# A hybrid decoder trunk on one core: the S5 loop's tile products moved to the end of the iteration, the next tile's matrix products put behind two weight units

## The chip, the core and the metric

The kernel runs on one core of one Trainium2 chip. The metric is device time in microseconds (us) of one execution; lower is better. The time before is 1483.97 us, the median of 3 runs (1483.57 to 1484.95). Engines are named as in the profile: PE (TensorE; PEld is its weight loads), DVE (VectorE), ACT (ScalarE), POOL (GpSimd) and SP (SyncE), which issues all of the kernel's DMAs.

## What is computed

One layer is applied to a prompt of 512 tokens and to 8 samples of 4 tokens, 544 columns in all. The normed input is projected to four branches of width 1024 (A: Mamba-2 SSD, B: S5, C: mLSTM, D: cross-attention); each branch goes through its own down projection, the four are merged by gates, and an output projection and a last norm follow. The change lies in branch B, the S5 scan: 64 groups of 16 channels with a complex state of 64 each.

```python
lam_bar = jnp.exp(lam * dt)
b_bar = ((lam_bar - 1.0) / lam)[..., None] * lax.complex(b_re, b_im)
bu = jnp.einsum('gnc,btgc->btgn', b_bar, ug)      # 16 channels -> 64 states
bu = bu.at[:, 0].add(lam_bar * h0)
h = lax.associative_scan(combine, (a_el, bu))      # h_t = lam_bar h_(t-1) + bu_t
y = jnp.einsum('gcn,btgn->btgc', c, h).real + d_skip * u
y = gelu(y)
```

## The kernel before, in words

**Weight units.** Nearly all of the matrix work is done by `unit` (the matmuls stand on L188): one unit multiplies 128 output columns of a weight with all 544 columns of the activations. A float32 product is made of three products of rounded parts, so a unit has 8 x 3 x 2 = 48 matmuls of 128x272. SP loads the weight block into `raw` (512 KB, three buffers), ACT rounds it into `whi` (L177), DVE subtracts to get `wlo` (L64), PE multiplies into the PSUM tile `pu` (two buffers). `gate_down` is a generator of such units: a gate unit (input `xh`, `xl`), then a down unit (input `oh`, `ol`) whose result DVE multiplies into `merged`. `step(gd, n)` runs n of them.

**The S5 loop** handles the 64 groups in 8 tiles f = 0..7 of 8 groups (128 channels), with the time axis cut into 64 chunks of 8 steps. Its parts, with the tiles that the profile names:
- `s5_in(f)`: one unit for the input columns of tile f; ACT and DVE copy `pu` to `uf`, which goes to DRAM (`ud`) and back as `U` in another layout (two DMAs).
- `s5_mats(f)`: DVE and POOL build the matrices `bm` (input to state) and `cm` (state to output); PE transposes `bm` into PSUM (`pbt`, L739), ACT and DVE copy that to `bt`; PE multiplies `cm` with `bbs` (`pk`, L768) for the short convolution inside a chunk, ACT copies it to `kt`, which goes to DRAM (`kd`) and back as `tp`.
- `s5_scan(f)`: PE makes `pvr` and `pvi` from `U` and `bt` (L791, 32 matmuls); DVE and POOL rotate them by the phases `E` (`gr`, `gi`, `t`), scan (L807, L808), rotate back to `hs`, and add the sample states to `hn`, which is the last reader of `pvr` and `pvi`.
- `s5_y(f)`: PE makes `py` from `tp` and `U` and from `cm` and `hs` (L846, L847, 32 matmuls); ACT copies `py` to `yj` (the same buffer as `uf`), which goes to DRAM (`yd`) and back as `yt`.
- `s5_out(f)`: PE permutes `yt` into PSUM (`pn`, L858 to L860); ACT and DVE apply the GELU to the stage tile `st`.
- `s5_rot(q)`, after the even iterations 0, 2 and 4: POOL alone builds the phases of the tiles 2q and 2q+1 by doubling (`rt`, `st`).

The small PSUM tiles (`pvr`, `pvi`, `pbt`, `pk`, `py`, `pn`) share four banks. The program builder hands the instructions to the engines by a timing model, so the order in the program is near that of the code but not the same, and matmuls of a unit stand on both sides of smaller work. Each engine then runs its own instructions strictly in that order.

Before, one iteration is written: scan of f, matrices of f+1, output of f-1, one unit of `gd`, `s5_y` of f, the input unit of f+2, one more unit of `gd` (none at f = 0 and f = 5).

Of the kernel before, what the change touches and what calls it, by code (L numbers as in the profile page):

```python
# [8 lines left out]
F32 = mybir.dt.float32  # L9
# [7 lines left out]
P = 128  # L17
# [17 lines left out]
def hybrid_kernel(ctx: ExitStack, tc: tile.TileContext, I, O):  # L35
    nc = tc.nc
    V, G, S, T = nc.vector, nc.gpsimd, nc.scalar, nc.tensor
# [7 lines left out]
    def ctile(shape, name, dt=F32):  # L45
        return cst.tile(shape, dt, name=name, tag=name)

    def bank(name="bk"):
        return pst.tile([P, 512], F32, name=name, tag="bk")
# [7 lines left out]
    def copy(eng, out, in_):  # L57
        if eng is S:
            S.copy(out, in_)
        else:  # L60
            eng.tensor_copy(out, in_)
# [39 lines left out]
    ident = ctile([P, P], "ident")  # L101
# [134 lines left out]
    def step(gen, n=1):  # L236
        for _ in range(n):
            next(gen, None)
# [4 lines left out]
    for c in range(5):  # L243
        n = P if c < 4 else TS
# [46 lines left out]
    pb = bank("pb")  # L291
# [11 lines left out]
    pb = bank("pb")  # L303
# [39 lines left out]
    for c in range(2):  # L343
# [8 lines left out]
        for hb in range(2):  # L352
            pb = bank("pmt")
# [4 lines left out]
            f = xm0.tile([P, 4, P], F32, name="mf", tag="mf")  # L358
# [71 lines left out]
    for b in range(NB):  # L430
# [10 lines left out]
        for h in range(4):  # L441
            kt_ = xk.tile([P, 2, 256], F32, name="kbt", tag="kbt", bufs=6)
            kts.append(kt_)
            pb = bank("pkt")
# [17 lines left out]
    pb = bank("pps")  # L462
# [51 lines left out]
    NV = 80  # L514
# [171 lines left out]
    pb = bank("pxo")  # L686
# [12 lines left out]
    s5r = s5c.enter_context(tc.tile_pool(name="s5r", bufs=1, side="right", reuse_waits="tile"))  # L699
# [8 lines left out]
    def s5_in(f):  # L708
        pu = unit(wcols(C_U + f * P), x2, perm=True)
        uf = s5r.tile([P, 8, NV], F32, name="uf", tag="uf", bufs=1)  # L710
        G.memset(uf[:, 4:8, 0:8], 0.0)
        G.memset(uf[:, 0:4, 72:80], 0.0)
        S.copy(uf[:, :, 8:42], pu[:, 0, 0:272].rearrange("p (k s) -> p s k", s=8))
        S.copy(uf[:, :, 42:72], pu[:, 1, 0:240].rearrange("p (k s) -> p s k", s=8))
        us = pu[:, 1, 240:272].rearrange("p (b t) -> p t b", t=4)
        V.tensor_copy(uf[:, 0:4, 0:8], us)
        V.tensor_copy(uf[:, 4:8, 72:80], us)
        U = s5r.tile([P, 8, NV], F32, name="U", tag="U", bufs=2)
        ud = s5d.tile([8, P, NV], F32, name="ud", tag="ud")
        dma(ud.rearrange("q p k -> p q k")[:, ::-1], uf)  # L720
        dma(U, ud.rearrange("q (c g) k -> (q c) g k", g=8))

        return U

    def s5_mats(f):
        gs = slice(4 * f, 4 * f + 4)

        def e4(a, m):
            return bc(a[:, 0:m, gs].rearrange("p l a -> p a l"), 3, 16)
        bm = s5r.tile([P, 2, 4, 8, 16], F32, name="bm", tag="bm")  # L730
        q1 = s5r.tile([P, 4, 9, 16], F32, name="q1", tag="sc1")
        q2 = s5r.tile([P, 4, 9, 16], F32, name="q2", tag="sc2")
        bbrf, bbif = bc(bbr[:, gs, :], 2, 8), bc(bbi[:, gs, :], 2, 8)
        cmul(V, G, bm[:, 0], bm[:, 1], e4(pwr, 8), e4(pwi, 8), bbrf, bbif, q1[:, :, 0:8, :], q2[:, :, 0:8, :])
        bt = s5r.tile([P, 2, 4, P], F32, name="bt", tag="bt")
        for ri in range(2):
            pb = bank("pbt")
            for a in range(4):
                T.transpose(pb[:, a * P:(a + 1) * P], bm[:, ri, a].rearrange("p l c -> p (l c)"), ident)  # L739
            copy(S if ri else V, bt[:, ri].rearrange("p a n -> p (a n)"), pb)  # L740

        cm = s5r.tile([P, 8, 9, 16], F32, name="cm", tag="cm", bufs=2)
        cmv = cm.rearrange("p (a b) l c -> p a b l c", b=2)
        ctrf, ctif = bc(ctr[:, gs, :], 2, 9), bc(cti[:, gs, :], 2, 9)
        q1 = s5r.tile([P, 4, 9, 16], F32, name="q1", tag="sc1")
        q2 = s5r.tile([P, 4, 9, 16], F32, name="q2", tag="sc2")
        tt(G, q1, e4(pwr, 9), ctrf, MUL)
        tt(V, q2, e4(pwi, 9), ctif, MUL)
        for g2 in range(2):
            pr = slice(64 * g2, 64 * g2 + 64)  # L750
            tt(V, cmv[0:64, :, g2], q1[pr], q2[pr], SUB)
        q1 = s5r.tile([P, 4, 9, 16], F32, name="q1", tag="sc1")
        q2 = s5r.tile([P, 4, 9, 16], F32, name="q2", tag="sc2")
        tt(G, q1, e4(pwi, 9), ctrf, MUL)
        tt(G, q2, e4(pwr, 9), ctif, MUL)
        for g2 in range(2):
            pr = slice(64 * g2, 64 * g2 + 64)
            stt(cmv[64:128, :, g2], q1[pr], -1.0, q2[pr], MUL, SUB)

        bbs = s5r.tile([P, 4, 2, 16], F32, name="bbs", tag="bbs", bufs=2)  # L760
        for ri, src in enumerate((bbr, bbi)):
            for g2 in range(2):
                dma(bbs[64 * ri:64 * ri + 64, :, g2, :], src[64 * g2:64 * g2 + 64, gs])

        pk = bank("pk")
        for g2 in range(2):
            for a in range(4):
                T.matmul(pk[32 * a:32 * a + 32, g2 * P:(g2 + 1) * P], bbs[:, a].rearrange("p g c -> p (g c)"),  # L768
                         cm[:, 2 * a + g2, 0:8, :].rearrange("p l c -> p (l c)"), start=True, stop=True,
                         tile_position=(0, 32 * a))  # L770
        kt = s5r.tile([P, 2, P], F32, name="kt", tag="kt")
        S.copy(kt.rearrange("p g x -> p (g x)"), pk[:, 0:256])
        stt(kt[:, :, 0:16], bc(i16, 1, 2), dcol[:, f:f + 1], kt[:, :, 0:16], MUL, ADD)

        kd = kds[f % 2]
        for a in range(4):
            dma(kd[:, a, :, 112:240], kt[32 * a:32 * a + 32])
        tp = [s5r.tile([P, 4, P], F32, name="tp", tag=f"tp{g2}", bufs=2) for g2 in range(2)]
        for g2 in range(2):
            dma(tp[g2], bass.AP(tensor=kd.tensor, offset=kd.offset + g2 * (16 * 1920 + 240),  # L780
                                         ap=[[16, 8], [1920, 16], [480, 4], [1, P]]))
        return bt, cm, tp, ev_[f // 2][:, :, f % 2]

    def s5_scan(f, U, bt, E):
        gs = slice(4 * f, 4 * f + 4)

        pv = [bank("pvr"), bank("pvi")]
        for g in range(8):
            pr = slice(64 * (g % 2), 64 * (g % 2) + 64)
            for ri in range(2):  # L790
                T.matmul(pv[ri][pr, (g // 2) * 72:(g // 2) * 72 + 72], bt[:, ri, g // 2, pr], U[:, g, 8:80],  # L791
                         start=True, stop=True)
# [44 lines left out]

    def s5_y(f, U, cm, tp, hs_):

        yj = s5r.tile([P, 8, 72], F32, name="yj", tag="uf")  # L840
        for hb in range(2):
            py = bank("py")
            for g4 in range(4):
                g = 4 * hb + g4
                o = py[:, g4 * 72:(g4 + 1) * 72]
                T.matmul(o, tp[g % 2][:, g // 2, :], U[:, g, 0:72], start=True, stop=False)  # L846
                T.matmul(o, cm[:, g, 1:9, :].rearrange("p l c -> p (l c)"), hs_[:, g, 0:72], start=False, stop=True)  # L847
            S.copy(yj[:, 4 * hb:4 * hb + 4, :].rearrange("p g k -> p (g k)"), py[:, 0:288])
        yt = s5r.tile([P, 8, 72], F32, name="yt", tag="yt")
        yd = s5d.tile([P, 8, 72], F32, name="yd", tag="yd")  # L850
        dma(yd, yj)
        dma(yt, yd.rearrange("(j c) g k -> (c g) j k", c=16))
        return yt
# [12 lines left out]
            S.activation(ga, ga, AF.Tanh)  # L866
            stt(ga, ga, 1.0, y, ADD, MUL)

    us_, mt_, yt = [s5_in(0)], s5_mats(0), None
    step(gd)  # L870
    us_.append(s5_in(1))
    step(gd)
    for f in range(8):
        bt, cm, tp, E = mt_
        hs_ = s5_scan(f, us_[f], bt, E)
        if f < 7:
            mt_ = s5_mats(f + 1)
        if f > 0:
            s5_out(f - 1, yt)
        step(gd)  # L880
        yt = s5_y(f, us_[f], cm, tp, hs_)
        if f < 6:
            us_.append(s5_in(f + 2))
        step(gd, (0, 1, 1, 1, 1, 0, 1, 1)[f])
        if f % 2 == 0 and f // 2 + 1 in range(1, 4):
            s5_rot(f // 2 + 1)
    s5_out(7, yt)
# [43 lines left out]
    with tc.tile_pool(name="sd", bufs=1, side="right", reuse_waits="tile") as sd:  # L931
# [199 lines left out]
        for q in range(3):  # L1131
            cvr = sr.tile([24, 512], F32, name="cvr", tag="M", bufs=1)
            dma(cvr, I["state_ssd_conv"][0].rearrange("b j c -> (b j) c")[:, q * 512:(q + 1) * 512])
            pb = bank("pcv")
# [33 lines left out]
        for g in range(2):  # L1168
            pb = bank("pbt")
# [3 lines left out]
            pb = bank("pcb")  # L1173
# [8 lines left out]
        for j in range(8):  # L1182
# [8 lines left out]
            pb = bank("pxt")  # L1191
# [9 lines left out]
            for h2 in range(2):  # L1201
                h = 2 * j + h2
                pb = bank("pac")
# [47 lines left out]
        for q in range(3):  # L1251
            pb = bank("pco")
# [28 lines left out]
        for g in range(2):  # L1281
            pb = bank("pbs")
# [10 lines left out]
        pb = bank("pms")  # L1293
# [9 lines left out]
        for hb in range(2):  # L1303
            pb = bank("pxs")
# [22 lines left out]
        for b in range(NB):  # L1327
# [5 lines left out]
            bm = sr.tile([96, 2, P], F32R, name="bmk", tag="bmk")  # L1333
# [5 lines left out]
            for hb in range(2):  # L1339
# [3 lines left out]
                pb = bank("pso")  # L1343
# [4 lines left out]
            for hb, so in enumerate(sos):  # L1348
                tt(G, so, so, bc(decS[:, 4 * hb:4 * hb + 4, b], 2, P), MUL)
                pb = bank("psn")  # L1350
# [7 lines left out]
        for qd in range(4):  # L1358
# [3 lines left out]
            for j in (2 * qd, 2 * qd + 1):  # L1362
                o = py[:, j * TS:(j + 1) * TS]
                a = 2 * (j % 2)
# [16 lines left out]
        pb = bank("pss")  # L1381
        for c in range(5):
            n = P if c < 4 else TS
# [6 lines left out]
        pb = bank("prb")  # L1390
# [4 lines left out]
        pb = bank("prb")  # L1395
# [13 lines left out]
    with tc.tile_pool(name="mlr", bufs=1, side="right", reuse_waits="tile") as mr:  # L1409
        for h in range(4):  # L1410
# [24 lines left out]
            for c in range(4):  # L1435
                sl = slice(c * P, (c + 1) * P)
                pb = bank("pkv")
# [42 lines left out]
            for dt in range(2):  # L1480
# [3 lines left out]
                pb = bank("pht")  # L1484
# [10 lines left out]
            pb = bank("pss")  # L1495
# [14 lines left out]
    with tc.tile_pool(name="mss", bufs=1, side="right", reuse_waits="tile") as ms:  # L1510
# [9 lines left out]
        for hb in range(2):  # L1520
            pb = bank("pk4")
# [16 lines left out]
        pb = bank("pqs")  # L1538
# [19 lines left out]
        pb = bank("pnr")  # L1558
# [5 lines left out]
        for b in range(NB):  # L1564
# [14 lines left out]
            for hb, cb in enumerate(cbs_):  # L1579
                for a in range(4):  # L1580
                    h = 2 * hb + a // 2
                    pb = bank("pcn")
# [4 lines left out]
        pb = bank("pnn")  # L1587
# [162 lines left out]
```

## Time and profile before

| | |
|---|---|
| median of 3 runs | 1483.97 us (1483.57 to 1484.95) |
| the profiled execution's own time | 1485.14 us |
| span of its trace | 1483.4 us, mean granted TensorE clock 0.98 |
| busy over the span | PE 1429.9 us (96%), DVE 888.4 (60%), ACT 490.5 (33%), POOL 344.5 (23%) |
| S5 loop, from the first `pvr` to the last `pn` | 277.37 to 503.2 us: 225.8 us |

The profile is of one execution, 1.2 us above the median. A row of its timeline has the start, the duration, the engine, the line, the operation, output<-input, the shapes, how many instructions are merged in it, and in square brackets how long the engine had been idle before it and what ended that. The table by stretches gives, for each, its length, the busy time of each engine, the granted TensorE clock (1.00 is full speed), the DMA share and the rate. A busy PE at a granted clock under 1.00 is a slower PE.

### The profile page before, as it was taken

To read this page: it belongs to the slowest core of one execution; us is meant where nothing else is said; L and a number is where in the kernel's file an instruction comes from. 1 tells how busy PE (TensorE), PEld (TensorE's weight loads), DVE (VectorE), ACT (ScalarE), POOL (GpSimd) and SP (SyncE) were. 2 spreads that over 40 slices of the span, in tenths; PEclk is the share of its full clock that TensorE was granted. 3 is DMA by queue.
4 is the path that set the end of the run, shared out by engine and by line. 5 is a ranking of instruction groups with operands and counts; after the bars stand their busy time and mean duration, and the time that the engine had idled before them with its cause. 6 is when DMAs were issued, how large, how long until landed. Compare 5 with 4: busy or idle time off the path is not lost. (4 is left out here: it accounts for less than half of the span.)

```text
span 1483.4 us, 28126 instructions
## 1 busy us (share of the span) xinstructions
PE 1429.9 (96%) x11505; PEld 1359.0 (92%) x11505; DVE 888.4 (60%) x1739; ACT 490.5 (33%) x849; POOL 344.5 (23%) x511
## 2 busy tenths in 40 slices
PE   6999998898999999999999999999999999899997
PEld 6998888888888999999999899999999998789997
DVE  5355587876887695677777544544343465454543
ACT  5244334223323432433333332433232332114332
POOL 2010233767572111002222222000000011110222
PEclk9999999989999999999999999999999999999999
DMA  8577362545545333322222464132323235663341
GB/s 204 164 224 227 108 195 64 125 107 134 122 96 129 84 86 90 86 72 76 75 73 76 111 187 136 50 87 60 91 65 86 71 110 173 204 197 109 100 146 61
DMA packets 298498, 172.92 MB, mean 117 GB/s; under 512 B 46365, under 2 KB 289385, under 8 KB 298370
## 3 DMA queue, kind: packets, MB, share of 16 engines
q1 hardware_dynamic: 298370, 171.14, 41.9%
q8 instruction: 90, 1.47, 0.4%
q14 instruction: 38, 0.31, 0.1%
HBM read 145.35 MB, written 25.24 MB: 115 GB/s over the span
## 5 line engine op out<-in xcount | busy, mean ns | idle before, releaser
L188 PE MATMUL pu<-xh,whi 128*128 128x272 f32 (+1 forms) x2000 | 431.4, 294 | 0.2 <-DVE hp L937 0.2
L188 PE MATMUL pu<-xl,whi 128*128 128x272 f32 (+1 forms) x2000 | 430.2, 293 | 0.1
L188 PE MATMUL pu<-xh,wlo 128*128 128x272 f32 (+1 forms) x2000 | 430.0, 294 | 0.0
L64 DVE TENSOR_TENSOR wlo<-raw,whi 128x1024 fp32r<-128x1024 f32 x181 | 249.7, 1380 | 223.9 <-ACT whi L177 219.9
L177 ACT CAST whi<-raw 128x1024 fp32r<-128x1024 f32 x181 | 198.6, 1097 | 485.4 <-PE pu L188 354.2
L188 PEld LDWEIGHTS pu<-xl,whi 128*128 128x128 f32 x2000 | 322.7, 192 | 5.5 <-issue 4.8
L188 PEld LDWEIGHTS pu<-xh,whi 128*128 128x128 f32 x2000 | 321.7, 191 | 6.4 <-issue 5.3
L188 PEld LDWEIGHTS pu<-xh,wlo 128*128 128x128 f32 x2000 | 321.2, 192 | 3.8 <-issue 3.5
L188 PE MATMUL pu<-ol,whi 128*128 128x272 f32 x640 | 136.4, 292 | 0.0
L188 PE MATMUL pu<-oh,whi 128*128 128x272 f32 x640 | 135.6, 291 | 0.0
L188 PE MATMUL pu<-oh,wlo 128*128 128x272 f32 x640 | 133.8, 289 | 0.0
L188 PEld LDWEIGHTS pu<-ol,whi 128*128 128x128 f32 x640 | 102.1, 190 | 1.8 <-issue 1.7
L188 PEld LDWEIGHTS pu<-oh,whi 128*128 128x128 f32 x640 | 101.8, 190 | 1.3 <-issue 1.0
L188 PEld LDWEIGHTS pu<-oh,wlo 128*128 128x128 f32 x640 | 101.2, 190 | 0.8 <-issue 0.7
L64 POOL TENSOR_TENSOR merged<-merged,gt 128x544 f32<-128x544 f32 x18 | 28.0, 1557 | 139.3 <-DVE gt L67 139.2
L67 DVE SCALAR_TENSOR_TENSOR cb<-cb,dcm,pcn 128x257 f32<-128x257 f32 x64 | 28.6, 479 | 26.3 <-PE pcn L1583 26.0
L67 DVE SCALAR_TENSOR_TENSOR cc<-cc,dcm,pcu 128x257 f32<-128x257 f32 x24 | 11.5, 479 | 44.6 <-PE pcu L1462 44.6
L188 PE MATMUL pu<-mh,whi 128*128 128x256 f32 x128 | 37.8, 296 | 0.1
L64 POOL TENSOR_TENSOR SS<-SS,dec 128x128 f32<-128x128 f32 x24 | 19.6, 815 | 77.6 <-DVE SS L1222 49.8
L188 PE MATMUL pu<-mlo,whi 128*128 128x256 f32 x128 | 37.1, 290 | 0.0
L188 PE MATMUL pu<-mh,wlo 128*128 128x256 f32 x128 | 36.3, 283 | 0.0
L1445 POOL MEMSET vtl<- 128x2 f32 x16 | 1.6, 99 | 143.3 <-PE pcu L1462 140.2
(638 smaller groups left out, 2278.2 us busy)
## 6 DMA issues: line engine op xcount, KB each, us to landing
raw<-in_w_in_dram SPq DMA_DIRECT2D x124, 512.0 KB
raw<-in_w_down_dram SPq DMA_DIRECT2D x32, 512.0 KB
kb<-in_cache_mem_k_dram SPq DMA_DIRECT2D x8, 1024.0 KB
raw<-in_w_mem_kv_dram SPq DMA_DIRECT2D x16, 512.0 KB
vb<-in_cache_mem_v_dram SPq DMA_DIRECT2D x16, 512.0 KB
cb<-in_state_mlstm_c_dram SPq DMA_DIRECT2D x16, 512.0 KB
out_dram<-cb SPq DMA_DIRECT2D x16, 512.0 KB
tp<-kd SPq DMA_DIRECT2D x16, 256.0 KB
```

Source lines behind the costliest of these rows:

```text
L64: eng.tensor_tensor(out, a, b, op)
L67: V.scalar_tensor_tensor(out, a, s, b, op0, op1)
L177: S.copy(hv, rv)
L188: T.matmul(ps[:, a, 0:c1 - c0], wt[:, k, :], xt[:, k, c0:c1], start=first, stop=last)
L1445: G.memset(vtl[:, 256:258].bitcast(F32), 0.0)
```

## The change

`s5_mats` is cut in two. What DVE and POOL do for `bm` and `cm`, and the loads of `bbs`, stay in `s5_mats`; the transposes `pbt`, the copies to `bt`, the products `pk` and the round trip `kt`, `kd`, `tp` become `s5_mats2`. In the loop, `s5_mats2(f + 1)` now stands behind a unit of `gd` and the input unit of f+2, and `s5_y(f)`, which used to stand in the middle, ends the iteration. `U` of tile f is therefore still needed when that of f+2 is loaded, and gets a third buffer. Nothing that is computed changes.

```diff
-        U = s5r.tile([P, 8, NV], F32, name="U", tag="U", bufs=2)
+        U = s5r.tile([P, 8, NV], F32, name="U", tag="U", bufs=3)
...
         for ri, src in enumerate((bbr, bbi)):
             for g2 in range(2):
                 dma(bbs[64 * ri:64 * ri + 64, :, g2, :], src[64 * g2:64 * g2 + 64, gs])
+        return bm, cm, bbs
+
+    def s5_mats2(f, bm, cm, bbs):
+        bt = s5r.tile([P, 2, 4, P], F32, name="bt", tag="bt")
+        for ri in range(2):
+            pb = bank("pbt")
+            for a in range(4):
+                T.transpose(pb[:, a * P:(a + 1) * P], bm[:, ri, a].rearrange("p l c -> p (l c)"), ident)
+            copy(S if ri else V, bt[:, ri].rearrange("p a n -> p (a n)"), pb)
...
-    us_, mt_, yt = [s5_in(0)], s5_mats(0), None
+    us_, yt = [s5_in(0)], None
+    mt_ = s5_mats2(0, *s5_mats(0))
...
         hs_ = s5_scan(f, us_[f], bt, E)
         if f < 7:
-            mt_ = s5_mats(f + 1)
+            ma = s5_mats(f + 1)
         if f > 0:
             s5_out(f - 1, yt)
         step(gd)
-        yt = s5_y(f, us_[f], cm, tp, hs_)
         if f < 6:
             us_.append(s5_in(f + 2))
+        if f < 7:
+            mt_ = s5_mats2(f + 1, *ma)
         step(gd, (0, 1, 1, 1, 1, 0, 1, 1)[f])
+        yt = s5_y(f, us_[f], cm, tp, hs_)
```

What this does to PE's order is seen in iteration f = 4. Before, from the last product of the scan to the first of `py` (`pu` rows are unit matmuls; the left-out rows are more of them):

```order
L791 MATMUL pvi<-U,bt 64x72
L739 MATMUL pbt<-ident,bm 128x128 x8
L188 MATMUL pu<-xh,whi 128x272 x2
...
L768 MATMUL pk<-cm,bbs 32x128 x8
L858 MATMUL pn_4790<-yt,permid 128x272
...
L859 MATMUL pn_4791<-yt,permid 128x240
L860 MATMUL pn_4791<-yt,permid 128x32
...
L846 MATMUL py<-U,tp 128x72
L847 MATMUL py<-hs,cm 128x72
```

Between `pvi` and `py` stand 59 unit matmuls, `pbt` follows the scan at once, and the other 85 unit matmuls of the iteration follow `py`. In the changed program, the same iteration:

```order
L794 MATMUL pvi<-U,bt 64x72
L188 MATMUL pu<-xh,whi 128x272 x2
...
L861 MATMUL pn_4757<-yt,permid 128x272
L862 MATMUL pn_4758<-yt,permid 128x240
L863 MATMUL pn_4758<-yt,permid 128x32
...
L765 MATMUL pbt<-ident,bm 128x128 x8
L771 MATMUL pk<-cm,bbs 32x128 x8
L188 MATMUL pu<-oh,whi 128x272 x2
...
L849 MATMUL py<-U,tp 128x72
L850 MATMUL py<-hs,cm 128x72
```

All 144 unit matmuls of the iteration now stand between `pvi` and `py`: 62 ahead of `pn`, 34 between `pn` and `pbt`, 48 between `pk` and `py`; the next scan follows `py` at once. At f = 2 `pn` has 54 ahead of it, at f = 3 and f = 5 it has 58.

On DVE, iteration f = 2 before. The names are those of the parts above; `q` are factors of `bm` and `cm`:

```order
L716 COPY uf<-pu 128x4x8
L717 COPY uf<-pu 128x4x8
L67 SCALAR_TENSOR_TENSOR cm<-q_4025,q_4026 64x4x144 x2
L64 TENSOR_TENSOR wlo<-raw,whi 128x8x8x16
L64 TENSOR_TENSOR gr<-st_2890,pvr 128x256
L64 TENSOR_TENSOR t_3951<-st_2890,pvi 128x256
L64 TENSOR_TENSOR gi<-st_2890,pvi 128x256
L64 TENSOR_TENSOR t_3952<-st_2890,pvr 128x256
L61 COPY bt<-pbt 128x512
L64 TENSOR_TENSOR bm<-pwr,bbr 128x512
L807 SCALAR_TENSOR_TENSOR gr<-rho_1830,gr 128x64 x4
L67 SCALAR_TENSOR_TENSOR kt<-i_1840,dcol,kt 128x2x16
```

The copies of `uf`, `bt` and `kt` stand inside or right ahead of the scan's chain. In the changed program, the same place:

```order
L64 TENSOR_TENSOR wlo<-raw,whi 128x8x8x16
L64 TENSOR_TENSOR cm<-q_4006,q_4007 64x4x144 x2
L64 TENSOR_TENSOR gr<-st_2890,pvr 128x256
L64 TENSOR_TENSOR t_3951<-st_2890,pvi 128x256
L64 TENSOR_TENSOR gi<-st_2890,pvi 128x256
L64 TENSOR_TENSOR t_3952<-st_2890,pvr 128x256
L67 SCALAR_TENSOR_TENSOR cm<-q_4012,q_4013 64x4x144 x2
L810 SCALAR_TENSOR_TENSOR gr<-rho_1830,gr 128x64 x4
L811 SCALAR_TENSOR_TENSOR gi<-rho_1830,gi 128x64 x4
...
L64 TENSOR_TENSOR hn<-hn,pvi 128x8x4
L61 COPY bt<-pbt 128x512
```

`bt` now follows the last reader of `pvi`, `uf` and `kt` follow `bt`, and one pair of `cm` stands ahead of the scans.

More of the change, by code (lines that the diff above doesn't have):

```diff
@@ L734, in s5_mats @@
         cmul(V, G, bm[:, 0], bm[:, 1], e4(pwr, 8), e4(pwi, 8), bbrf, bbif, q1[:, :, 0:8, :], q2[:, :, 0:8, :])
[L735 to L740, printed above, removed]
         cm = s5r.tile([P, 8, 9, 16], F32, name="cm", tag="cm", bufs=2)
```

## The prediction

> **What bounds the kernel now.** I read the table by stretches first. It splits the span into the S5 loop and what follows it:
>
> ```profile
> 277.37:503.20 225.83, 208.46 (x1738) 193.05 (x1738) 172.56 (x342) 70.67 (x135) 131.99 (x202) 0.94 0.50 116
> 503.20:800.00 296.80, 296.13 (x2412) 291.88 (x2410) 216.24 (x409) 104.27 (x150) 51.28 (x57) 1.00 0.29 80
> ```
>
> Columns: length, then busy time of PE, PEld, DVE, ACT and POOL, granted clock, DMA share, GB/s. After the loop PE is busy 296.13 of 296.80 us at full clock, so nothing is to be had there. In the loop PE lacks 17.4 us of 225.83, and its clock is 0.94. PE is the bound; what the change can win are PE's gaps and the slow clock around them, in the loop alone.
>
> The same table with one stretch per iteration, cut at the first `pvr` of each:
>
> ```profile
> core 0: us, PE busy (x) PEld busy (x) DVE busy (x) ACT busy (x) POOL busy (x), PEclk, DMA share, GB/s
> 277.37:303.02 25.65, 22.05 (x185) 21.26 (x184) 17.36 (x36) 6.15 (x12) 22.59 (x43) 0.87 0.69 151
> 303.02:335.86 32.84, 29.16 (x240) 26.56 (x239) 27.73 (x48) 9.23 (x18) 19.43 (x17) 0.90 0.38 96
> 335.86:370.01 34.15, 30.39 (x239) 28.32 (x238) 23.95 (x47) 10.21 (x21) 25.87 (x50) 0.90 0.54 128
> 370.01:399.14 29.13, 26.94 (x240) 25.14 (x239) 24.30 (x47) 9.66 (x19) 14.40 (x14) 1.00 0.50 119
> 399.14:431.90 32.76, 30.66 (x239) 28.50 (x238) 26.37 (x47) 9.34 (x19) 27.02 (x48) 0.90 0.48 109
> 431.90:455.05 23.15, 21.10 (x192) 19.19 (x191) 18.99 (x40) 7.80 (x16) 10.95 (x10) 1.00 0.47 106
> 455.05:476.03 20.98, 20.98 (x191) 19.10 (x190) 15.11 (x38) 6.37 (x15) 5.51 (x9) 1.00 0.54 135
> ```
>
> Iterations f = 1 to 4 have three units, f = 0, 5 and 6 two. f = 6 runs without a gap: 20.98 us is what two units and the small products cost. Length minus PE's busy time gives idle of 3.60, 3.68, 3.76, 2.19, 2.10 and 2.05 us in f = 0 to 5: 17.4 us. The clock takes 13% of 25.65 (3.3 us), and 10% each of 32.84, 34.15 and 32.76 (3.3, 3.4, 3.3): 13.3 us. All that the change can win is 17.4 + 13.3 = 30.7 us.
>
> What ends the gaps, by PE's timeline:
>
> ```profile
> 292.87 0.44 PE L847 MATMUL py<-hs,cm 128*128 128x72 f32 x2 [3.60 <-DVE hs L64]
> 319.20 0.66 PE L768 MATMUL pk<-cm,bbs 128*32 128x128 f32 x8 [3.68 <-issue]
> 342.70 0.64 PE L768 MATMUL pk<-cm,bbs 128*32 128x128 f32 x16 [1.42 <-ACT bt L59]
> 355.97 0.44 PE L846 MATMUL py<-U,tp 128*128 128x72 f32 x2 [1.40 <-DVE st L67]
> 389.86 0.44 PE L846 MATMUL py<-U,tp 128*128 128x72 f32 x2 [2.19 <-DVE st L67]
> ```
>
> All are small S5 products which stand on PE before what they read, or the bank they write, is ready: `py` waits for `hs` or for the GELU to free its bank, `pk` for a copy of `pbt`. Units wait behind them.
>
> **Why DVE comes late.** In f = 2 the scan's products are made at 335.86, but:
>
> ```profile
> 339.39 0.39 ACT L713 COPY uf<-pu 128x272 f32<-128x272 f32 x1 [5.28 <-DMA yd<-yj]
> 340.07 0.19 DVE L716 COPY uf<-pu 128x32 f32<-128x32 f32 x1 [3.38 <-ACT uf L714]
> 344.29 0.42 DVE L64 TENSOR_TENSOR gr<-st,pvr 128x256 f32<-128x256 f32 x1
> 356.38 0.17 DVE L64 TENSOR_TENSOR hn<-hn,pvi 128x32 f32<-128x32 f32 x1
> ```
>
> `uf` shares its buffer with `yj`, so its copy waits for the `yd` transfer; DVE stands 3.38 us behind that copy, and `gr` starts 8.4 us after the scan's products began. From there to the last `hn` it is 12.3 us.
>
> **The change part by part.** PE's prices, from its timeline:
>
> ```profile
> 252.79 0.42 PE L188 MATMUL pu<-xh,wlo 128*128 128x272 f32 x2
> 253.04 0.41 PE L188 MATMUL pu<-xh,whi 128*128 128x272 f32 x2
> 337.06 1.09 PE L739 MATMUL pbt<-ident,bm 128*128 128x128 f32 x8
> 377.31 1.14 PE L858 MATMUL pn<-yt,permid 128*128 128x272 f32 x2
> ```
>
> Two unit matmuls start every 0.25 us, so a unit of 48 takes 6.0 us. The scan's products take 1.2 (335.86 until `pbt` at 337.06), `pbt` 1.0, `pn` 1.14 for half of its columns, about 2.0 in all. A gap-free iteration is then 20.98 us with two units and 27.0 with three. No matmul is added or removed; the sum is what idle and clock loss are left of 30.7.
>
> *f = 2 to 5, the scan's cover.* `py` now has all units ahead of it (18 us, 12 at f = 5), so `hs` is no longer waited for. The first to wait is `pbt`: it needs a free bank, which `hn` or the GELU gives. Ahead of it on PE stand the scan (1.2), two units (12.0) and `pn` (2.0): it comes 15.2 us after the scan starts. DVE's chain takes 12.3 us; it loses `bt`, `kt` and a `bm` product and gains a pair of `cm`:
>
> ```profile
> L61 DVE COPY bt<-pbt 128x512 f32<-128x512 f32 x7 | 4.8, 685 | 0.0
> L67 DVE SCALAR_TENSOR_TENSOR kt<-i,dcol,kt 128x32 f32<-128x32 f32 x7 | 2.6, 369 | 0.0
> L67 DVE SCALAR_TENSOR_TENSOR cm<-q,q 64x576 f32<-64x576 f32 x14 | 11.1, 794 | 3.9 <-POOL q L64 3.5
> ```
>
> That is -0.69 - 0.37 - 0.7 + 1.59, about zero. And `uf` of f+2 is now copied an iteration after `yd` was sent, so the 3.38 us in front are gone. If DVE is at `gr` when the scan ends (1.2), `hn` is done at 13.5, 1.7 us ahead of `pbt`. If it is late by the largest gap that now stands at f = 3, 2.19 are left. I take the middle, 1.1 us each in four iterations: 4.4 us, bounds 0 and 8.8. Clock loss: none taken, since f = 3 and f = 5 have idle of 2.19 and 2.05 at clock 1.00.
>
> *f = 0.* The cover grows from 67 unit matmuls to 97 (12.1 us), but DVE is behind:
>
> ```profile
> 281.88 2.19 DVE L64 TENSOR_TENSOR wlo<-raw,whi 128x1024 fp32r<-128x1024 f32 x1
> 282.00 2.30 POOL L64 TENSOR_TENSOR rt<-st,pw 128x8 f32<-128x8 f32 x2 [1.72 <-DVE cm L67]
> 291.44 1.83 DVE L64 TENSOR_TENSOR hs<-t,t 64x256 f32<-64x256 f32 x4
> 294.69 1.21 DVE L64 TENSOR_TENSOR wlo<-raw,whi 128x1024 fp32r<-128x1024 f32 x1
> ```
>
> `hs` is done at 293.3. In the new order `bt`, a `bm` product and `kt` leave the chain, while a `merged` and a `wlo` (1.21) enter it: about 293 again. PE is through its two units and `pbt` at 277.37 + 1.2 + 12.0 + 1.0 = 291.6, then waits for that `wlo`, and after `pk` for `hs`: 2.0 us idle, between 0 and today's 3.60.
>
> *f = 1.* `s5_rot(1)` keeps POOL until 301.1, and DVE's `q` waits for it:
>
> ```profile
> 299.70 1.41 POOL L64 TENSOR_TENSOR st<-st,rt 128x256 f32<-128x256 f32 x2
> 301.14 1.59 DVE L64 TENSOR_TENSOR q<-pwi,bbr 128x512 f32<-128x512 f32 x1 [4.61 <-POOL st L64]
> 304.04 1.30 POOL L64 TENSOR_TENSOR bm<-bm,q 128x512 f32<-128x512 f32 x1
> 307.89 0.43 DVE L64 TENSOR_TENSOR gr<-st,pvr 128x256 f32<-128x256 f32 x1
> ```
>
> In the new order `gr` still stands behind `q`, behind this `bm` (done at 305.3) and one more `q` (about 0.8): 306.1 is the earliest, and `hn` is done at 318.4. PE starts this scan at 277.37 + 19.0 + 2.0 + 1.7 = 300.1 (19.0: 20.98 without `pn`) and reaches `pbt`, with 8 unit matmuls more ahead of it, at 300.1 + 16.2 = 316.3: 2.1 us idle, between 0 and 3.68. For the clock of f = 0 and f = 1 I take half of today's 3.3 each, 3.3 together, bounds 0 and 6.6.
>
> *Third `U` buffer, the split of `s5_mats`, later `kt` and `tp`.* `tp` of f+1 is read a whole iteration after it is sent; nothing on PE waits, cost zero by that cover. f = 6 and the code after the loop: zero.
>
> **Sum.** Left: 4.4 + 2.0 + 2.1 + 3.3 = 11.8 us. Gain: 30.7 - 11.8 = 18.9. The profiled execution's 1485.14 becomes 1466.2; the median stands 1.17 lower: 1465.1. With all bounds at their good end the gain is 30.7.
>
> The clock is the doubtful term. In f = 2 no gap is above 1.42 us, yet its clock is 0.90. The Trainium skill, "TensorE: Matmul & The Clock Gate", section "HAM oscillation — how this bites in real kernels", has only idle gaps beyond about 3.4 us cost the clock; f = 3 agrees, f = 2 does not. By that rule the 3.3 us would go and the time be about 1461.8.
>
> **The rivals.**
>
> *All stalls go.* For it: 1.7 us of slack in f = 2 to 5. Against: DVE and POOL were behind already in f = 0 and f = 1. With 2 us left: 1483.97 - 28.7 = 1455.3. Chance 0.22.
>
> *DVE and POOL become the bound.* They slow each other: `wlo` takes 2.19 us beside POOL's `rt` and 1.21 alone. In f = 4 POOL is busy 27.02 us, as long as a gap-free iteration, DVE 26.37; every wait between the two then shows. If f = 0, 2 and 4, with `s5_rot` on POOL, gain nothing and f = 1, 3 and 5 two thirds of their 7.0, 2.2 and 2.05, the gain is 7: 1477. Chance 0.18. The Trainium skill, "SBUF — State Buffer", section "SBUF: two separate sides", says of the port pair which the two engines share that it is "an exclusive lock, not a bandwidth split"; the two `wlo` rows agree.
>
> *Slower: the `yt` round trip.* Between the last `py` and `pn` stood at least 57 unit matmuls beside the scan, `pbt` and `pk` (at f = 5), some 10 us; now it is the scan and 54 to 62 unit matmuls, 8.0 to 9.0 us, in f = 2 to 5. The trip:
>
> ```profile
> 332.78 0.40 ACT L848 COPY yj<-py 128x288 f32<-128x288 f32 x1 [1.20 <-PE py L847]
> 333.21 1.86 SPq L851 DMA_DIRECT2D yd<-yj  x1
> 339.37 0.37 SPq L852 DMA_DIRECT2D yt<-yd  x1
> 493.19 0.40 ACT L848 COPY yj<-py 128x288 f32<-128x288 f32 x1 [1.34 <-PE py L847]
> 495.86 0.37 SPq L852 DMA_DIRECT2D yt<-yd  x1
> 501.06 1.14 PE L858 MATMUL pn<-yt,permid 128*128 128x272 f32 x2
> ```
>
> From `yj` to the issue of `yt` it took 6.6 us here, 2.7 at the loop's end; `yt` itself at most 5.2 (`pn` did not wait there). At the longest, 11.8 us: late by 3.3 in four iterations, each with the 3.3 of clock that f = 0 shows for a gap of 3.60: 26 us, plus the 7.4 of f = 0 and f = 1, is 34 against 30.7: 1487. It decides once the trip is over about 11.4 us each time. Chance 0.07.
>
> *No change.* PE's wait only moves from `py` to `pbt` and `pn`: 1484. Chance 0.05.
>
> **How the numbers follow.** The forecast has 0.48: 1465.1, its own range 1460 to 1470 (left 6.7 to 16.7). The range from the rivals *all stalls go* and *DVE and POOL* is 1455 to 1478; it leaves out 0.12 and some edges. Within 0.2% (3 us, about what a measurement here can tell from no change) lies only *no change*. Faster 0.48 + 0.22 + 0.18 = 0.88, same 0.05, slower 0.07.
>
> **What would show it.** Right: no `py` row with a gap ended by `hs` or `st` in f = 2 to 6, `gr` within 2 us of the scan's end, iterations of 27 to 29 us with three units, clock 1.00 from f = 2 on, no copy of `uf` waiting for `yd`. Wrong: gaps before `pbt` ended by `hn` or `st` (DVE late), before `pn` with no engine as releaser (the trip), or a clock still at 0.90 with gaps under 1.5 us.

## The result and the profile after

The changed kernel is slower: 1498.76 us median of 6 runs (1494.45 to 1502.27) against 1484.46 (1481.28 to 1489.69) of the kernel before beside it, a ratio of 1.009 with a 95% interval of 1.0069 to 1.0111. The profiled execution took 1497.04 us, its span is 1495.3 us. Lines are now: `pbt` L765, `pk` L771, `py` L849 and L850, `yd` L854, `yt` L855, `pn` L861 to L863. The ratios below leave out one execution of run e9, which took 2741 us.

I cut both traces where the same work starts and ends, from the first product of the scan to the first `pdec` behind the loop, with 2085 matmuls between (one record more in the first). Before, then after, in the table by stretches:

```profile
277.37:546.70 269.33, 251.96 (x2086) 236.40 (x2085) 207.66 (x390) 88.34 (x163) 137.01 (x205) 0.95 0.47 111
```

```profile
277.63:561.12 283.49, 251.94 (x2085) 240.13 (x2084) 206.39 (x390) 88.11 (x163) 128.98 (x205) 0.92 0.44 106
```

The stretch is 14.16 us longer, PE's busy time the same to 0.02 us. PE's idle time, length minus busy, went from 17.37 to 31.55 us: that is the whole loss. (The rest of the span came out 2.3 us shorter.) The table of waits of the changed kernel, in the loop, names the idle time: engine, line, releaser, total us, times, longest:

```profile
PE pn L861 <- DMA yt<-yd: 23.1, 6, 6.5
PE pk L771 <- DVE hn L64: 4.3, 1, 4.3
PE pu L188 <- DVE zz L67: 2.7, 1, 2.7
PE pbt L765 <- DVE hn L64: 1.3, 1, 1.3
```

No `py` row is left in it: the waits that the change was forecast to end did end. In their place `pn` waits in six of eight iterations for `yt`, without an engine as releaser. Two of the six in PE's timeline:

```profile
347.85 1.29 PE L861 MATMUL pn<-yt,permid 128*128 128x272 f32 x2 [5.68 <-DMA yt<-yd]
...
382.83 1.29 PE L861 MATMUL pn<-yt,permid 128*128 128x272 f32 x2 [6.48 <-DMA yt<-yd]
```

The trip of tile 2, which ends at that second `pn`: first ACT's copy, then SP's rows:

```profile
367.73 0.40 ACT L851 COPY yj<-py 128x288 f32<-128x288 f32 x1 [0.37 <-PE py L850]
```

```profile
367.34 0.55 SPq L721 DMA_DIRECT2D U<-ud  x1
368.07 1.30 SPq L783 DMA_DIRECT2D tp<-kd  x2
369.41 3.06 SPq L82 DMA_DIRECT2D raw<-in_w_in_dram  x2
372.52 2.88 SPq L854 DMA_DIRECT2D yd<-yj  x1
379.78 0.37 SPq L855 DMA_DIRECT2D yt<-yd  x1
```

`yj` is done at 368.13. SP then issues two `tp` and two weight loads and comes to `yd` at 372.52, 4.39 us later; the issue itself takes 2.88; `yt` can only be sent at 379.78, 7.26 after `yd`; `pn` starts 3.05 after that. The trip is 14.70 us; PE had work for 8.22 of it (382.83 - 6.48 - 368.13). The same tile before:

```profile
361.29 0.35 SPq L851 DMA_DIRECT2D yd<-yj  x1
363.44 0.36 SPq L852 DMA_DIRECT2D yt<-yd  x1
366.77 0.38 SPq L82 DMA_DIRECT2D raw<-in_w_in_dram  x1
368.52 0.36 SPq L720 DMA_DIRECT2D ud<-uf  x1
```

There `yd` left 0.03 us behind `yj`, the weight load and the input came after `yt`, and `yd` took 2.15 us. The last two columns of the table by stretches (DMA share, GB/s) during `yd`, before and after:

```profile
361.30:363.50 2.20, 2.20 (x12) 2.20 (x11) 1.32 (x2) 1.76 (x5) 1.57 (x2) 0.50 0.35 134
```

```profile
372.50:379.80 7.30, 3.85 (x31) 3.64 (x30) 6.08 (x16) 1.66 (x2) 4.33 (x4) 0.97 0.96 205
```

On this tile the DMA engines were 35% busy before and are 96% busy now: 1.5 MB pass in those 7.3 us (205 GB/s), of which `yd` is 288 KB. Over the six tiles with a gap SP's wait is 1.1 to 4.7 us (16.6 in all), `yd` 5.7 to 7.3, `yt` until `pn` 3.0 to 3.2, the trip 10.3 to 14.7, against 7.7 to 8.9 us of PE work. The mean DMA share during `yd` is 0.92 to 0.96 on tiles 2 to 4, and 0.52 to 0.68 on tiles 1, 5 and 6, where `yd` still took 5.7 to 6.0 us: the share alone does not give its time. A slow `yd` is not new either: before it took 2.2 to 6.2 us, but SP sent it 0.02 to 0.03 us behind `yj` on every tile, and PE had 7.3 to 20.9 us of work for the trip.

### The profile page after: what moved, and what is told of

It is laid out like the page before. It is cut to its first block, busy times and chain, and to the rows that moved or that the text cites. A ratio compares the mean times of both kernels' runs of the same rounds, so it can differ in the third digit from the quotient of the medians.

```text
span 1495.3 us, 28128 instructions
## 1 busy us (share of the span) xinstructions
PE 1428.6 (96%) x11505; PEld 1361.9 (91%) x11505; DVE 887.8 (59%) x1739; ACT 490.3 (33%) x849; POOL 336.9 (23%) x511
## 5 line engine op out<-in xcount | busy, mean ns | idle before, releaser
L64 DVE TENSOR_TENSOR wlo<-raw,whi 128x1024 fp32r<-128x1024 f32 x181 | 253.5, 1401 | 226.9 <-ACT whi L177 222.0
```

The costliest lines, as they stand in the source:

```text
L64: eng.tensor_tensor(out, a, b, op)
```

## The experiments

My theory: `yd`, which the change puts behind the input's, the matrices' and the units' transfers, is late both at SP and in the DMA engines, and PE, with less work between `py` and `pn`, stands for the difference. Rivals: the shorter cover alone; a late DVE that `pn` only happens to show; the clock, which the equal busy time of PE above already speaks against.

All runs in one table. Idle is PE's idle time in the stretch defined above (17.4 before, 31.6 after); the next columns are the parts of it that `yt` ends at `pn`, and that `hn` or the GELU's `st` ends at `pbt` and `pk`. A ratio is to the kernel before on the same chip.

| run | edit to the changed kernel | ratio (95%) | idle | `pn` | `hn`, `st` |
|---|---|---|---|---|---|
| (the change) | none | 1.009 (1.0069-1.0111) | 31.6 | 23.1 | 5.6 |
| e1 | output later | 1.004 (1.0021-1.0059) | 26.0 | 11.6 | 11.2 |
| e2 | `yd` from ACT | 0.9983 (0.9962-1.0005) | 21.9 | 12.7 | 6.3 |
| e7 | `yd`, `yt` from ACT | 1.0005 (0.9981-1.0029) | 22.6 | 12.6 | 6.0 |
| e10 | `hn` early | 1.010 (1.0063-1.0137) | 35.1 | 26.1 | 2.5 |
| e12 | e7 and e1 | 1.0007 (0.9988-1.0027) | 22.0 | 4.2 | 15.9 |
| e13 | e7 and e10 | 1.0012 (0.9995-1.003) | 21.3 | 14.7 | 2.8 |
| e11 | e7, e1 and e10 | 0.9956 (0.994-0.9972) | 15.4 | 2.3 | 3.5 |
| e5 | `kd`, `tp` sent later | 1.0052 (1.0027-1.0077) | 34.7 | 25.5 | 5.6 |
| e3 | only `py` moved | 1.0022 (1.0005-1.0039) | 26.9 | 9.9 | 0 |
| e4 | only the matrices moved | 1.0017 (0.9999-1.0036) | 21.1 | 0 | 0 |
| e8 | no weight loads | single run | 19.9 | 8.1 | 10.5 |
| e15 | no `kd`, `tp` | single run | 18.4 | 8.1 | 6.5 |
| e16 | neither | single run | 18.4 | 0 | 15.7 |
| e9 | the kernel before, `yd` from ACT | 0.9999 (0.9976-1.0022) | 17.8 | 0 | 0 |

### e2_yd_act: another queue for yd

```diff
-        dma(yd, yj)
+        S.dma_start(yd, yj)
```

> The changed kernel with the yd transfer issued by ScalarE, right behind its own yj copies, instead of by SyncE, where it stood 1.1 to 4.7 us behind the issue of the other loads. Theory A (the queue at SyncE makes the trip long): the pn gaps fall by that wait, to about 1, 2, 1.2, 1.8, 0.2 and 0.3 us, 23.1 become about 7, time about 1480. Theory B (the transfers ahead of yd in the DMA engines make it long, 5.7 to 7.3 us for the yd transfer itself): yd lands about when it did, the transfer from issue to landing takes longer than 7 us, the pn gaps keep over 16 of 23.1 us, time above 1492. Rival (DVE late): as in the changed kernel, 1495 to 1500.

By the two ratios it is some 16 us under the changed kernel. `yd` leaves 0.03 us behind `yj` on every tile; the idle time at `pn`:

```profile
PE pn L861 <- DMA yt<-yd: 12.7, 6, 4.6
```

10.4 of 23.1 us are gone, not the 16 that theory A expected: in five of the first six tiles `yt` still follows `yd` by 5.6 to 6.6 us (theory B's part), and `yt` itself still stands in SP's queue. Tile 2:

```profile
365.07 4.97 SPq L82 DMA_DIRECT2D raw<-in_w_in_dram  x2
370.09 2.22 SPq L855 DMA_DIRECT2D yt<-yd  x1
```

So SP's queue is a little less than half of this wait; the runs without loads below are about the rest. The Trainium skill, "DMA: Bandwidth & Descriptors", section "Issuing engines are not separate DMA queues", says that issuing from several engines saves only the issue time, "which is usually small relative to the DMA itself". The trace fits shared DMA engines, since `yd` sent by ACT still took 5.6 to 6.6 us; but the time saved was not small here: SP's wait was up to 4.74 us of a trip of 13.4.

### e9_before_yd_act: the control

The same edit in the kernel before:

```diff
-        dma(yd, yj)
+        S.dma_start(yd, yj)
```

> A control: the kernel before with yd issued by ScalarE. There SyncE sent yd at most 1.1 us after yj in the iterations looked at, and pn had over 10 us of cover. Theory (the other queue only undoes what the change did): within 3 us of the kernel before, 1484 to 1490 on this chip's scale. Rival (ScalarE's queue is better for yd in any kernel, and the 14 us that it gave the changed kernel are no measure of the change's harm): 5 us or more faster than the kernel before.

0.9999: no difference. ACT's queue is no gain of its own, and what it gave in e2 undoes what the change did. The theory's row held.

### e1_out_later: more cover

```diff
-        if f > 0:
-            s5_out(f - 1, yt)
         step(gd)
         if f < 6:
             us_.append(s5_in(f + 2))
+        if f > 0:
+            s5_out(f - 1, yt)
```

> The changed kernel with the output products of f-1 put behind the input of f+2, so that pn stands behind 96 unit matmuls instead of 54 to 62 in iterations 2 to 5 (4.3 to 5.3 us more cover), and behind 55 instead of 74 in iteration 6. Theory (the trip yj, yd, yt takes 10.3 to 14.7 us against 8 to 9 us of cover, and PE stands at pn for the rest): the six pn gaps of 5.68, 6.48, 2.84, 3.90, 2.81 and 1.40 us become about 0.4, 1.7, 0, 0, 5.2 and 1.7, 23.1 us become 9; with some of the clock regained about 1475 to 1485 us, pn gaps named by yt<-yd only. Rival (DVE and POOL come late, and pn is only where it shows): the idle time turns up before pbt or pk instead, ended by hn or st, and the time stays above 1493. Rival (the clock, not the gaps): clock in the loop stays near 0.91 though the gaps are gone, and the time falls by 14 at most, to about 1485.

`pn`'s idle time halved, as expected in kind (11.6 for 9), but 1.004 is far from 1475 to 1485 us, since `pbt` now comes too early for `hn`:

```profile
PE pn L861 <- DMA yt<-yd: 11.6, 5, 4.4
PE pbt L765 <- DVE hn L64: 6.9, 3, 3.8
PE pk L771 <- DVE hn L64: 4.3, 1, 4.3
```

The late DVE is therefore real, and was covered by the wait at `pn`: the first theory holds in part, but it is not the only one. On tiles 2 and 4 `yd` now left 7.1 us behind `yj`, and the trip grew to 17.4 and 15.7 us. The clock rival finds no more support: the stretch's clock stayed at 0.92, and PE's busy time was 253.72 us.

### e8_no_loads, e15_no_tp, e16_neither: what stands ahead of yd

e8 makes `load` return one block loaded ahead of the loop (and gives `raw` two buffers for three, to make room for it); e15 returns the first tile's `tp` before `kd` is sent; e16 does both. The parts of the computation left out are in the expectations.

```diff
     def load(w):
+        if kept:
+            return kept[0]
...
+        if tps:
+            return bt, cm, tps[0], ev_[f // 2][:, :, f % 2]
         kd = kds[f % 2]
```

> The changed kernel with the units' weight loads left out in the S5 loop: all units there use one block of weights loaded ahead of the loop, so their results are of other weights. PE, DVE, ACT and POOL do the same work. yd stays on SyncE. Theory (the weight loads are what stands ahead of yd, at SyncE and in the transfers): SyncE's wait for yd under 1.5 us, yd itself under 3.5 us, the trip 6 to 8 us, pn gaps under 2 us in all. Rival (the matrices' and the input's own transfers): yd still 5 to 7 us, pn gaps over 12 us. Rival (cover too short in any case): pn gaps over 12 us though the trip is under 8 us. The idle before pbt and pk that hn ends (5.6 us) stays in all three; the time of the whole is of no use, since the first units after the loop have to wait for their loads.

> The changed kernel with the kd and tp transfers left out after the first tile: every tile uses the tp of tile 0, so its results are of another matrix. The weight loads and the input's ud and U stay, and yd stays on SyncE behind them. Theory (the weight loads are most of what stands ahead of yd: without them pn's gaps fell from 23.1 to 8.1 us): yd still takes over 5 us, pn gaps over 14 us. Rival (the matrices' transfers do as much): yd under 4.5 us, pn gaps under 10 us.

> The changed kernel with both left out in the loop: no weight loads, no kd and tp; only the input's ud and U and the small bbs are left beside yd and yt. It asks for the trip with next to nothing in its way, at the cover that the change leaves. Theory (the cover of 8 to 9 us would do for a free trip): SyncE's wait under 0.7 us, yd 2.5 to 4 us, the trip under 8 us, pn gaps under 2 us. Rival (the cover is too short in any case): pn gaps over 8 us.

Leaving out either group of transfers takes `pn`'s idle time to 8.1 us, so e15's theory (the weight loads are most of it) is refuted: the two are worth about the same, each some 15 of 23 us, and they do most of the harm only together. e8's own theory (under 2 us) missed as well: SP's wait fell to 1.0 to 1.5 us on the three tiles for which `pn` waits, but `yd` took 5.6 to 6.4 there. In e15 `yd` took 4.3 to 4.5 us on tiles 2 to 4; most of what is left of the idle time (7.3 of 8.1 us, tiles 2 and 4) is one weight load that stands at SP until its buffer is free, with `yd` behind it. Tile 2:

```profile
359.12 0.34 SPq L721 DMA_DIRECT2D U<-ud  x1
365.89 0.37 SPq L82 DMA_DIRECT2D raw<-in_w_in_dram  x1
366.36 0.70 SPq L859 DMA_DIRECT2D yd<-yj  x1
```

In e16 the trip has a free road. Tile 2:

```profile
361.95 0.34 SPq L863 DMA_DIRECT2D yd<-yj  x1
364.06 0.37 SPq L864 DMA_DIRECT2D yt<-yd  x1
```

`yd` takes 2.1 to 2.2 us on five of eight tiles, and `pn` waits for `yt` nowhere: from `yj` to `pn` it is 7.3 us on five tiles, less than the 7.7 to 8.9 us of cover in the changed kernel. The rival of the short cover alone falls. But the idle time is 18.4 us all the same, and the one execution took 1483.53 us beside 1484.69 of the kernel before:

```profile
PE pbt L771 <- DVE st L67: 11.4, 3, 5.2
PE pk L777 <- DVE hn L64: 4.3, 1, 4.3
PE pu L192 <- DVE zz L67: 2.7, 1, 2.7
```

With the trip out of the way the idle time is where my second rival put it, at DVE. DVE in e16 at the end of iteration 2 and in iteration 3, whose scan products are done at 362.69:

```profile
358.79 1.59 DVE L64 TENSOR_TENSOR q<-pwi,bbr 128x512 f32<-128x512 f32 x1 [4.75 <-POOL st L64]
...
368.12 0.42 DVE L64 TENSOR_TENSOR gr<-st,pvr 128x256 f32<-128x256 f32 x1
370.69 2.49 DVE L67 SCALAR_TENSOR_TENSOR cm<-q,q 64x576 f32<-64x576 f32 x2 [1.16 <-POOL q L64]
...
382.93 0.18 DVE L64 TENSOR_TENSOR hn<-hn,pvi 128x32 f32<-128x32 f32 x1
```

POOL, which `s5_rot` holds until then, makes DVE late by 4.75 us before the matrices are begun; `gr` starts at 368.12, 5.4 us after the scan, and the last `hn` ends at 383.11, 15.0 us later and not the 12.3 that I had.

### e10_hn_early, e12_act_out_later, e13_act_hn, e11_best: the edits together

e10 moves the block that computes `hn` ahead of the recurrences (the first part of the diff); e7 issues `yd` and `yt` from ACT (the second); e12 is e7 with e1's order, e13 e7 with e10's block, e11 all three.

```diff
         tt(G, gi, gi, t2, SUB)
+        p4 = (bc(pwr[:, 4, gs], 1, NB), bc(pwi[:, 4, gs], 1, NB))
...
+        tt(V, hni, hni, vv[1][:, :, 64:72].rearrange("p a b -> p b a"), ADD)
         for a in range(4):
...
-        dma(yd, yj)
-        dma(yt, yd.rearrange("(j c) g k -> (c g) j k", c=16))
+        S.dma_start(yd, yj)
+        S.dma_start(yt, yd.rearrange("(j c) g k -> (c g) j k", c=16))
```

> The changed kernel with both yd and yt issued by ScalarE. Against the kernel with only yd there (pn gaps 12.7 us, 1484.8 us): yt no longer waits for a place among SyncE's issues, where one took 2.22 us in iteration 2. Theory (SyncE's queue is what is left of the loss): the pn gaps fall to 8 us or less, time 1477 to 1482. Rival (the transfers themselves are what is left): pn gaps 10 to 13 us, time within 3 us of 1485. Rival (the wait for yd's landing now holds ScalarE, and the weight copy whi stands behind it): gaps before the unit's products ended by ACT whi, time 1487 or more.

> The changed kernel with one edit that the change doesn't have: hn is computed ahead of the scan's recurrences on DVE, so that the banks which pbt and pk take come free some 8 us earlier. It undoes the 5.6 us that PE waits for hn. Theory (the trip is the loss, hn a smaller one beside it): no gap ended by hn above 1 us, pn gaps still 18 us or more, time 3 to 6 us under the changed kernel's 1498.8. Rival (a late DVE is the loss and pn only shows it): pn gaps under 10 us and time below 1488.

> The fastest of these kernels so far (yd and yt from ScalarE, output products later, hn early: 0.9956 of the kernel before) without the early hn. Theory (with the trip hidden, the late hn is the next thing that PE waits for): pn gaps under 4 us, gaps at pbt and pk ended by hn of 8 to 12 us, ratio to the kernel before 0.998 to 1.003. Rival (the early hn plays no part, the trip was all): ratio 0.994 to 0.997.

> The changed kernel with yd and yt issued by ScalarE and the early hn, the output products left where the change put them; it completes the set of the three edits. Without the early hn this kernel stood at 1.0005 of the kernel before, with 12.6 us of pn gaps and 6.0 ended by hn. Theory (each of the three edits is worth its own gaps, and hn's show once pn's are short): hn's 6.0 us go, pn keeps 12 to 15, ratio 0.996 to 0.999. Rival (the early hn gives nothing unless the output products come later, as it gave nothing in the changed kernel, since pn waits the longer for what pbt waits the less): pn gaps 15 us or more, ratio 0.9995 to 1.002.

> The changed kernel with yd and yt issued by ScalarE, the output products of f-1 behind the input of f+2 (13.2 us of cover for a trip of 10 to 12), and the additions of hn moved ahead of the scan's recurrences, so that the banks that pbt takes come free earlier. Theory (the trip and the late hn are all that the change lost by): pn gaps under 2 us and pbt and pk gaps under 2 us in the loop, clock 0.97 or more there, time 15 to 25 us under the kernel before. Rival (DVE and POOL are the bound once the trip is gone): the idle time comes back before py, pk or a unit, ended by hs, cm or wlo, over 10 us in all, time no more than 5 us under the kernel before.

e7 fits its first rival (the transfers are what is left): `yt` on ACT as well makes no difference that shows. In e10 the waits for `hn` are gone and nothing is won, 1.010:

```profile
PE pn L862 <- DMA yt<-yd: 26.1, 7, 6.6
PE py L851 <- DVE hs L64: 3.1, 1, 3.1
PE pk L771 <- DVE st L67: 2.5, 1, 2.5
```

PE got to `pn` sooner, and waited there; `hs`, now behind `hn` on DVE, is late once. So a late DVE was not the cause of the loss. In e12 the trip is nearly hidden (4.2 us) and the waits for `hn` are at their largest (15.9 us, over the 8 to 12 expected):

```profile
PE pbt L765 <- DVE hn L64: 11.6, 3, 5.4
PE pk L771 <- DVE hn L64: 4.3, 1, 4.3
```

e13 has the early `hn` without the later output: 1.0012, `pn` 14.7 us. Its rival held in the time; only `pn` stayed just under the 15 us that it named. Only with all three, e11, does the idle time fall below that of the kernel before, and the time with it, 0.9956 (0.994 to 0.9972), some 6.5 us under it (the medians lie 4.0 apart):

```profile
PE pu L188 <- DVE wlo L64: 3.7, 1, 3.7
PE pbt L765 <- DVE hn L64: 3.5, 4, 1.2
PE pu L188 <- DVE zz L67: 2.8, 1, 2.8
PE pn L862 <- DMA yt<-yd: 2.3, 3, 0.9
```

That is neither the theory (15 to 25 us, clock 0.97; it was 0.95) nor quite the rival (over 10 us ended by `hs`, `cm` or `wlo`, at most 5 us won): with 3.1 us at `py`, 13 us of its idle time are ended by DVE. Each of the three edits removes a wait that another one uncovers; none of them alone, nor the two pairs that were run, beat the kernel before by more than the interval.

### e3_y_end_only, e4_mats2_only: the parts of the change

e3 calls `s5_mats2` right behind `s5_mats`, in its old place, and keeps `s5_y` at the end; e4 keeps `s5_y` in the middle and moves only `s5_mats2`. The first diff is e3's, the second e4's:

```diff
         if f < 7:
-            ma = s5_mats(f + 1)
+            mt_ = s5_mats2(f + 1, *s5_mats(f + 1))
...
-        if f < 7:
-            mt_ = s5_mats2(f + 1, *ma)
```

```diff
         step(gd)
+        yt = s5_y(f, us_[f], cm, tp, hs_)
         if f < 6:
...
-        yt = s5_y(f, us_[f], cm, tp, hs_)
```

> Only one part of the change: the output products py end the iteration and the input has three buffers, but the matrices are made whole at their old place, pbt and pk ahead of the units and kd and tp sent there, half an iteration ahead of yd. PE has about the same cover between py and pn as in the changed kernel (scan, pbt, 41 unit matmuls, pk: about 8.5 us). Theory (transfers of the matrices ahead of yd): yd leaves within 2 us of yj, the pn gaps sum to under 6 us, while the pk and pbt gaps of the kernel before come back (3 to 9 us in all); time 1470 to 1485. Rival (the cover alone is too short, whoever's transfers are about): pn gaps over 15 us, time 1490 or more.

> Only the other part of the change: pbt, pk, kt, kd and tp of f+1 stand behind the input of f+2, while the output products py stay in the middle of the iteration, where they were before. Theory (py at the iteration's end is what puts yd behind other issues and shortens pn's cover): yd within 2 us of yj, pn gaps under 5 us in all; what is left idle is before py (hs, st) as in the kernel before, or before the scan's products, which now follow pbt closely; 1485 to 1495. Rival (the moved transfers of the matrices alone make the trip long): pn gaps over 15 us, time above 1495.

Neither part alone does more than a quarter of the harm: 1.0022 and 1.0017. In e3 `yd` leaves within 1.8 us of `yj` and the trip is 6.3 to 10.3 us on the tiles for which `pn` waits, so it loses 9.9 us, between the two expectations; `pk` also waits once for 7.8 us, ended by nothing that the profile names. In e4 (whose profiled execution took 1497.9 us, 10 over its median, so that its idle time is a rough figure) `pn` waits for `yt` nowhere, but `py`, with one unit of cover, waits longer for the GELU's bank:

```profile
PE py L849 <- DVE st L67: 14.0, 6, 4.4
```

### e5_tp_behind_y: no answer

The calls that send `kd` and `tp` of f+1 are cut off `s5_mats2` and written behind `s5_y(f)`.

```diff
         yt = s5_y(f, us_[f], cm, tp, hs_)
+        if f < 7:
+            cm, tp = ma[1], s5_tp(f + 1, kt)
```

> The changed kernel with the kd and tp transfers of f+1 issued behind yd and yt of f instead of ahead of them; pbt, pk and kt stay where the change put them. Theory (the moved transfers of the matrices are what makes yd late): yd is issued within 2 us of yj, takes under 5 us, the pn gaps fall from 23.1 to under 10 us, time 1478 to 1487. Rival (the input's transfers ud, U, the unit's loads and bbs, which were there before, do it): SyncE's wait and the yd transfer stay within 1 us of what they were, pn gaps over 17 us, time above 1492. In both, py of f+1 reads tp an iteration later and should not wait for it.

The ratio is 1.0052 (1.0027 to 1.0077) and `pn` waits 25.5 us, which looks like the rival's case. But SP's rows show that the edit did not move what it was to move: the program builder put `tp` ahead of `yd` again in iterations 1 to 4.

```profile
365.00 1.30 SPq L786 DMA_DIRECT2D tp<-kd  x2
366.34 3.83 SPq L82 DMA_DIRECT2D raw<-in_w_in_dram  x2
370.22 2.70 SPq L857 DMA_DIRECT2D yd<-yj  x1
```

In iterations 5 and 6, where one of two `tp` did go behind `yd`, SP's wait fell by 0.7 and 0.8 us and the gap at `pn` by 0.7 and 0.9. As a whole it does not answer the question; e15 took its place.

## Why the prediction was wrong, point by point

**What can be won, and the waits at `py`: right.** PE's idle time is the whole difference, and all waits for `hs` and `st` before `py` are gone. One reading was not shown: the 3.68 us before `pk` at f = 1 have no releaser in the profile (`issue`), so a copy of `pbt` was a guess there.

**The zero-cost term failed.** For the third `U` buffer, the split of `s5_mats` and the later `kt` and `tp` the sum has "nothing on PE waits, cost zero by that cover". That asked who waits for the moved transfers, and found nobody soon. It did not ask what now stands behind them: `yd`, at SP and in the DMA engines; so the sum has no term for `pn` waiting for `yt`, although a rival had priced it. That is 23.1 us, which e2, e8, e15 and e16 each take away in part or whole. The stretch became 14.2 us longer where 18.9 less were forecast; of these 33.1 us, 23.1 are this wait and 10.0 the clock term below.

**The rival was right in mechanism and wrong in size.** It named place and releaser, and 8.0 to 9.0 us of cover (7.7 to 8.9). Its longest trip, 11.8 us, was put together from trips of the kernel before: the slowest `yd` there (6.2 us, tile 1, at a DMA share of 0.60), sent at once, and up to 5.2 for `yt`. Measured were 1.1 to 4.7 us of waiting at SP, 5.7 to 7.3 for `yd` and 3.0 to 3.2 for `yt`, 10.3 to 14.7 in all. So the part that it put at nothing is SP's wait. Its 13.2 us of idle time in f = 2 to 5 were 18.9, with 4.2 more in f = 6 and 7, while the clock loss that it added for each gap did not show in PE's busy time. It had a chance of 0.07, and 1498.8 lies 12 us beyond its 1487.

**The DVE terms hold by accident.** 2.0 us at f = 0 was 4.3, 2.1 at f = 1 was 1.3, 4.4 before `pbt` in f = 2 to 5 was 0, and 2.7 behind the loop had been put at zero: 8.3 measured for 8.5. But the waits at `pn` gave DVE that time. Without them (e16) `pbt`, `pk` and the unit behind the loop wait 18.4 us: in f = 3 and 5, behind an `s5_rot` on POOL, `gr` starts 5.4 to 5.5 us after the scan's end and the chain to `hn` is 15.0 us and not 12.3. The 12.3 of f = 2 was the shortest of f = 2 to 5: in f = 3 to 5 of the kernel before it was 12.9 to 16.1, in f = 2 to 5 of the changed one 14.4 to 17.8. My second rival's mechanism would have been next; by that one run the change with a free trip is about level with the kernel before.

**The clock term failed too.** I counted 10 of 13.3 us as regained. The granted clock of the stretch fell from 0.95 to 0.92, and in no kernel here did PE's busy time fall by more than 2.8 us (e3, 249.17 for 251.96). Of the 22.2 us of clock lost in the changed kernel (13.7 before), 4.1 fell where PE was idle anyway (0.8 before). Why its busy time stayed the same although it lost more of the clock while busy, 18.1 for 12.8 us, stays open.

## What to carry to other kernels

Price a moved transfer by what it is put in front of, in its issuer's queue and in the DMA engines, and not only by who waits for its data. A round trip through DRAM is no constant: the same 288 KB took 2.1 us with the DMA engines a third busy and 7.3 with them 96% busy, and 6.2 us once in the kernel before, where its cover hid it. So the cover has to be sized for the place to which the trip moves. And a large wait hides the next one: before forecasting what is left when a stall goes, find the second-latest arrival at the same place.

## What the runs showed of the hardware

The clock came in steps that I had not expected. Summed over stretches of 0.5 us, every drop goes to half speed and costs 1.7 us of clock or a multiple of it: four of 3.4 us before; one of 5.1, four of 3.4 and two of 1.7 after. They also begin on a grid: worked out from these stretches, the four before begin at 293.61, 317.51, 358.47 and 416.49, which is 7, 12 and 17 times 3.41 us apart, and the seven after 14, 10, 10, 9, 9 and 7 times 3.41. One of the 1.7, behind the shortest of the six gaps at `pn` (columns: length, PE busy, and third from the end the clock):

```profile
494.94:496.34 1.40, 0.00 (x1) 0.03 (x1) 1.40 (x5) 0.66 (x1) 0.00 (x0) 1.00 0.52 125
496.34:498.50 2.16, 2.16 (x7) 1.17 (x8) 2.16 (x8) 0.40 (x1) 0.00 (x0) 1.00 0.44 119
498.50:502.00 3.50, 3.50 (x19) 3.50 (x19) 2.37 (x6) 1.98 (x5) 0.00 (x0) 0.55 0.25 77
```

Only 1.40 us without work stand ahead of this drop, and half speed came some 2.5 us after PE was busy again, at the next point of the grid (498.87); before, 2.19 us of idle time cost nothing:

```profile
387.50:390.00 2.50, 0.31 (x3) 0.14 (x2) 2.47 (x9) 0.71 (x2) 0.00 (x0) 1.00 0.61 140
390.00:394.00 4.00, 4.00 (x36) 4.00 (x37) 2.10 (x6) 1.36 (x4) 0.11 (x1) 1.00 0.95 197
```

The length of a single gap does not decide it. Counted by steps of the grid at full clock in the two traces, idle time of 1.98 us or more in one step was followed by half speed each time (seven of seven), 0.7 to 1.93 us in four of fourteen, less never; what decides between the fourteen is not shown. The steps agree with the window of some 3.4 us of the Trainium skill, "TensorE: Matmul & The Clock Gate", section "Part 1: The HAM clock gate (the "warmup" mystery)". The same page's rule "no PE-idle gaps >~3.4µs", section "HAM oscillation — how this bites in real kernels", is too lenient here: five of the eleven drops came behind gaps that were all shorter than 3.4 us. So what a gap costs beyond its own length goes in steps, and shorter gaps need not win the clock back.
